# Corrected durations in the planner that orders the instruction streams of a hybrid decoder step

## The chip, the cores and the metric

The kernel runs on one core of one Trainium2 chip. The metric is the device time of one execution in microseconds (us). A core has five engines with a queue each: TensorE (PE) multiplies matrices, VectorE (DVE) and ScalarE (ACT) work element by element, GpSimd (POOL) does the same more slowly and issues the gathers, SyncE (SP) issues most DMAs. Each engine takes its instructions strictly in the order in which the program was written, and waits on semaphores where an operand isn't ready. Matmuls read SBUF and write PSUM, which this kernel uses as eight banks of 128x512 float32.

## The reference

One step of a decoder layer, for a prompt of 1024 tokens and for 8 decode samples of one token with 1024 cached positions:

```python
h = rms_norm(x, norm_g) * (1.0 + scale) + shift          # adaLN of c
proj = h @ w_in                                          # q, 6 k/v, gates, z_a, u, v, z_b, g_a, g_b
o_c, o_s, o_w = nsa_core(...)    # compressed, top-8 selected blocks of 64, window of 512; per-head gates
s_b = spatial_mix(vn, w_s, b_s)  # causal mix in chunks of 128
a = (o_a * silu(z_a)) @ w_br_a
b = (u * s_b * silu(z_b)) @ w_br_b
m = sigmoid(g_a) * a + sigmoid(g_b) * b
y = x + gate * (m @ w_out)
```

Beside y it returns the new K/V rows, the window buffers and the normalised v rows. The samples gather their cached K/V pages by a page table. All is float32.

## The kernel before, in words

Float32 accuracy comes from splitting an operand into a rounded high part and a low remainder (names ending in h and l), and multiplying three times (high by high, high by low, low by high) in the form `float32r`. These are the "split" matmuls of the change. Transposes and a few small products run in plain float32 ("full"), and 16 products of a raw 512-column weight slice with the 9 columns of c ("part" in the change) open the program (`mm<-graw,cT`, `mm<-araw,cT`).

The work has these stages, in the order of the profile:

- Start: the weights of the adaLN are streamed in, x is normalised, transposed and modulated into hh and hl.
- Projections: vg, k, q and v of the prompt (`bh`, `bl`, `gh`, `gl` are their split weights).
- Decode (names gk, gw, kh, kl, psT): for 8 samples, key and value pages of 512 KB are gathered by POOL into four buffers `gk`. For each sample PE transposes the eight 128x128 blocks of a gathered key page in two groups of four (`mx<-main,gk`), ACT rounds each group (`kh<-mx`), DVE takes the remainder (`kl`), and two 512-column matmuls (`st<-kh,qpad`, `st<-kl,qpad`) give the scores. DVE also sums the compressed pages (`red<-gk`). Then come the window pages (`gw`), a softmax, and the products with the values.
- Attention of the prompt: 16 tiles of 128 queries (two groups of heads, eight blocks). Per tile a front part (maxima of the scores by `mx<-L,R` matmuls that DVE reduces into `bm` and `wm`, then the selection), and per span of 128 keys a score pair (`st<-R,L`), an exponential on ACT (`pt<-st`), a mask on POOL, the split into p, and three matmuls on V (`pv<-p,vv`). A tile is closed by sums that go out through DRAM and come back (`sr`, `s`, `w_d`, `f`), a product `mx<-pgT,vc`, and a store to `o_d`.
- Merge: `xh`, `xl` are the split products of z and o (`zt<-z_db`, `zx<-o_d`), multiplied with w_br_b and w_br_a (matmuls `xh,c0h` and so on), gated, summed, split again; then the output projection (`oh`, `ol`).

Beside decode and attention runs a stream of independent jobs, the filler: the projections u, z_a, z_b and the 16 gates, 28 jobs of three pieces. A piece is 24 split matmuls of 344 columns on hh and hl with a chunk of weights (`mm<-hh,c0h`, `mm<-hl,c0h`, `mm<-hh,c0l`; c1 for every other chunk), offered six matmuls at a time, with a tanh on ACT at its end (`th<-mm`) and a store (`t_da<-th` for the last gates). There are 84 pieces, and the merge can't start before all of them are issued, since it is the next job of the same stream.

What decides the order of all this is the class `Plan`. The source is a set of Python generators, one for each stream. As each instruction is written out, `Plan.op` books it on a model of its engine with a duration from `Plan.cost`, and so keeps for each engine the time at which it is free and for each tile the time at which it is ready. `Plan.go` picks, at each step, the generator to continue: first those whose next operand the model calls ready by the time the model's PE is free, among these the one of lowest rank. The filler has rank 9, so it is taken when nothing else is ready in the model. The function `paced` limits the filler during attention by the share of spans done. Nothing of this runs on the chip: the model only fixes in which order the instructions stand in the queues. Every instruction is written out through one line of `Plan.engine`, line 217, so all rows of the profile carry L217.

Of the kernel before, what the change touches and what calls it, by code (L numbers as in the profile page):

```python
# [9 lines left out]
F32 = mybir.dt.float32  # L10
FR = mybir.dt.float32r
BF = mybir.dt.bfloat16
# [16 lines left out]
class Pack:  # L29


    def __init__(self):
        self.cols, self.parts, self.n = {}, [], 0
# [59 lines left out]
class Plan:  # L93
# [6 lines left out]
    def __init__(self):  # L100
        self.free, self.bus, self.slots, self.rings, self.seen = {}, 0.0, {}, {}, {}
        self.columns, self.streams, self.last = {}, [], 0.0
        self.gone, self.since, self.spilled = 0.0, {}, {}

    def tile(self, pool, uid, shape, dtype, name, bufs=1):
        t = pool.tile(shape, dtype, name=name, tag=name, bufs=bufs)
        n = self.rings.get((uid, name), 0)
        self.rings[uid, name] = n + 1
        self.slots[t.tensor.name] = (uid, name, n % bufs)
        return t  # L110
# [54 lines left out]
    def cost(self, engine, name, outs, ins, size, start):  # L165
        if engine == "pe":
            n, m, dt = ins[1].free_size(), ins[0].free_size(), ins[0].dtype
            cost, passes = max(n / 2.4 + 2.5, (26 if dt == BF else 104) * m / 128), 1
            if name == "transpose":
                passes = 2  # L170
            elif dt == F32:
                cost, passes = max(4 * n / 2.4, 208 * m / 128), 4
            tick = int(start // self.TICK)
            self.columns[tick] = self.columns.get(tick, 0.0) + passes * n * ins[0].partition_size() / 128
            return cost * (2 if self.cold(start) else 1)
        if engine == "dve":
            plain = name == "tensor_copy" and outs[0].space == ins[0].space
            return 67 + (0.52 if plain else 1.042) * size
        if engine == "act":
            return (280 if len(ins) > 1 else 70) + 0.834 * size  # L180
        if name == "affine_select":
            return 65 + 1.4 * size
        if name == "tensor_scalar":
            return max(330 + 0.83 * size, 3.61 * size - 28)
        return (300 + 165 * size if size < 16 else 70 + 2.27 * size)
# [1836 lines left out]
```

## Time and profile before

| | |
|---|---|
| median of 3 runs | 1063.16 us (1062.73 to 1066.06) |
| profiled execution | 1060.27 us, its span 1058.5 us |
| PE busy | 1010.8 us (95%) |
| DVE, ACT, POOL busy | 693.9 us (66%), 469.2 us (44%), 307.6 us (29%) |
| granted TensorE clock, mean | 0.991 |

Time idle on PE is what to look for: where PE is busy at full clock, only its own work counts. A row of a timeline gives the start and the length of an instruction; matmuls overlap, so their pitch is the difference of two starts. A table of windows gives the busy time of each engine in a stretch, and the granted clock as a share of 2.4 GHz.

### The profile page before, as it was taken

What the parts mean: (1) busy time and instruction counts of PE and PEld (TensorE: products, weight loads), DVE (VectorE), ACT (ScalarE), POOL (GpSimd) and SP (SyncE); (2) the same over time, 40 slices, a digit from 0 to 9 for tenths busy, and PEclk for the clock granted to TensorE, in tenths of its full rate; (3) what the DMA queues carried; (4) which work ended last, traced back from release to release, by engine and by line L of the source; (5) the groups of instructions that cost most, each with busy time, mean ns of one, the idle gap of its engine ahead of it and who ended that gap; (6) DMA issues with size and microseconds to landing.
All of it is one profiled execution on the core that took longest, in us unless ns stands there. A gap on an engine that the chain in (4) does not pass through costs nothing. (4 is left out here: it accounts for less than half of the span.)

```text
span 1058.5 us, 16280 instructions
## 1 busy us (share of the span) xinstructions
PE 1010.8 (95%) x5587; PEld 875.9 (83%) x5587; DVE 693.9 (66%) x1507; ACT 469.2 (44%) x984; POOL 307.6 (29%) x332
## 2 busy tenths in 40 slices
PE   7999999999999999999999999998999859999998
PEld 2589977879999999988886788877878849998776
DVE  5677786344668665679789867989774146674322
ACT  5763332002222255667765666765776232232000
POOL 0453565463321110013433222342434200252000
PEclk9999999999999999999999999999999979999999
DMA  9726360115766654421322121111112278553421
GB/s 329 260 85 193 115 198 31 60 36 162 261 193 194 223 174 157 129 63 60 86 61 60 61 61 46 55 61 43 36 49 61 81 230 251 169 178 123 139 89 62
DMA packets 106312, 130.33 MB, mean 123 GB/s; under 512 B 27299, under 2 KB 71525, under 8 KB 106230
## 3 DMA queue, kind: packets, MB, share of 16 engines
q1 hardware_dynamic: 101622, 112.52, 33.5%
q0 software_dynamic: 4608, 16.78, 5.2%
q8 instruction: 44, 0.72, 0.3%
q14 instruction: 38, 0.31, 0.1%
HBM read 98.95 MB, written 30.23 MB: 122 GB/s over the span
## 5 line engine op out<-in xcount | busy, mean ns | idle before, releaser
L217 PE MATMUL pv<-p,vv 128*128 128x512 f32 (+1 forms) x396 | 112.7, 400 | 3.5 <-ACT p L217 2.1
L217 PE MATMUL mm<-hh,c0h 128*128 128x344 f32 x328 | 107.7, 328 | 0.0
L217 PE MATMUL mm<-hl,c0h 128*128 128x344 f32 x328 | 105.2, 321 | 0.0
L217 PE MATMUL mm<-hh,c0l 128*128 128x344 f32 x328 | 105.2, 321 | 0.0
L217 PE MATMUL mm<-hh,c1h 128*128 128x344 f32 x320 | 104.3, 326 | 0.0
L217 PE MATMUL mm<-hl,c1h 128*128 128x344 f32 x320 | 102.1, 319 | 0.0
L217 PE MATMUL mm<-hh,c1l 128*128 128x344 f32 x320 | 102.1, 319 | 0.0
L217 ACT ACTIVATE pt<-st 128x512 f32<-128x512 f32 x132 | 78.6, 595 | 50.2 <-PE st L217 45.2
L217 PEld LDWEIGHTS pv<-p,vv 128*128 128x128 f32 (+1 forms) x396 | 65.9, 172 | 27.2 <-DVE p L217 2.6
L217 PE MATMUL st<-R,L 128*128 128x512 f32 (+1 forms) x264 | 85.5, 405 | 0.0
L217 DVE TENSOR_TENSOR p<-pt,p 128x512 fp32r<-128x512 f32 x88 | 67.1, 770 | 12.6 <-ACT p L217 12.1
L217 POOL TENSOR_TENSOR p<-pt,p 128x512 fp32r<-128x512 f32 x44 | 58.9, 1340 | 56.2 <-ACT p L217 49.7
L217 ACT ACTIVATE p<-pt 128x512 fp32r<-128x512 f32 x94 | 59.1, 629 | 14.0 <-POOL pt L217 11.6
L217 PEld LDWEIGHTS mm<-hh,c0h 128*128 128x128 f32 x328 | 62.3, 190 | 2.9 <-issue 0.2
L217 PEld LDWEIGHTS mm<-hh,c0l 128*128 128x128 f32 x328 | 62.2, 190 | 2.6
L217 PEld LDWEIGHTS mm<-hh,c1h 128*128 128x128 f32 x320 | 60.2, 188 | 2.7 <-issue 0.2
L217 PEld LDWEIGHTS mm<-hh,c1l 128*128 128x128 f32 x320 | 60.2, 188 | 2.5
L217 PEld LDWEIGHTS mm<-hl,c0h 128*128 128x128 f32 x328 | 62.1, 189 | 0.0
L217 POOL TENSOR_SCALAR_AFFINE_SELECT pt<-pt 128x512 f32<-128x512 f32 x40 | 27.1, 678 | 116.0 <-ACT pt L217 99.0
L217 PE MATMUL mx<-L,R 128*128 128x512 f32 (+3 forms) x204 | 54.2, 336 | 6.7 <-DVE wm L217 3.0
L217 PEld LDWEIGHTS mm<-hl,c1h 128*128 128x128 f32 x320 | 60.1, 188 | 0.0
L217 ACT ACTIVATE th<-mm 128x344 f32<-128x344 f32 x69 | 31.3, 454 | 52.0 <-PE mm L217 51.7
(489 smaller groups left out, 2657.5 us busy)
## 6 DMA issues: line engine op xcount, KB each, us to landing
t_db<-th SPq DMA_DIRECT2D x24, 172.0 KB
t_da<-th SPq DMA_DIRECT2D x24, 172.0 KB
th<-t_db SPq DMA_DIRECT2D x24, 172.0 KB
th<-t_da SPq DMA_DIRECT2D x24, 172.0 KB
graw<-in_w_ada_dram SPq DMA_DIRECT2D x16, 256.0 KB
araw<-in_w_ada_dram SPq DMA_DIRECT2D x16, 256.0 KB
xt<-in_x_dram SPq DMA_DIRECT2D x8, 512.0 KB
eraw<-in_w_ada_dram SPq DMA_DIRECT2D x16, 256.0 KB
```

The costliest lines, as they stand in the source:

```text
L217: r = getattr(real, name)(*args, **kw)
```

## The change

The constants of `Plan.cost` are replaced, and the model keeps which form the last matmul had, with a time for each change of form. Nothing else in the source is changed. The diff:

```diff
--- before.py
+++ after.py
@@ -101,6 +101,7 @@
         self.free, self.bus, self.slots, self.rings, self.seen = {}, 0.0, {}, {}, {}
         self.columns, self.streams, self.last = {}, [], 0.0
         self.gone, self.since, self.spilled = 0.0, {}, {}
+        self.form = "split"
 
     def tile(self, pool, uid, shape, dtype, name, bufs=1):
         t = pool.tile(shape, dtype, name=name, tag=name, bufs=bufs)
@@ -165,19 +166,32 @@
     def cost(self, engine, name, outs, ins, size, start):
         if engine == "pe":
             n, m, dt = ins[1].free_size(), ins[0].free_size(), ins[0].dtype
-            cost, passes = max(n / 2.4 + 2.5, (26 if dt == BF else 104) * m / 128), 1
-            if name == "transpose":
-                passes = 2
-            elif dt == F32:
-                cost, passes = max(4 * n / 2.4, 208 * m / 128), 4
+            form, passes, turn = "split", 1, 0.0
+            if dt == FR and name != "transpose":
+                cost = max(0.4375 * n + 7, 104 * m / 128)
+                turn = {"split": 0.0, "full": 85.0, "part": 190.0}[self.form]
+            elif name == "transpose" or dt == BF:
+                form, passes = "full", 2 if name == "transpose" else 1
+                cost = max(0.4375 * n + 7, (26 if dt == BF else 104) * m / 128)
+                turn = 190.0 if self.form == "part" else 0.0
+            elif m <= 64 and n > 128:
+                form, passes, cost = "part", 4, 0.4375 * n * 4 * m / 128 + 3
+                turn = 0.0 if self.form == "part" else 140.0
+            else:
+                form, passes, cost = "full", 4, max(4 * (0.4375 * n + 7), 208 * m / 128)
+                turn = 190.0 if self.form == "part" else 0.0
+            self.form = form
             tick = int(start // self.TICK)
             self.columns[tick] = self.columns.get(tick, 0.0) + passes * n * ins[0].partition_size() / 128
-            return cost * (2 if self.cold(start) else 1)
+            return cost * (2 if self.cold(start) else 1) + turn
         if engine == "dve":
             plain = name == "tensor_copy" and outs[0].space == ins[0].space
+            if name == "reciprocal":
+                return 80 + 18 * size
             return 67 + (0.52 if plain else 1.042) * size
         if engine == "act":
-            return (280 if len(ins) > 1 else 70) + 0.834 * size
+            moved = ins and self.box(ins[0])[1][0] != self.box(outs[0])[1][0]
+            return (280 if len(ins) > 1 else 70) + 0.834 * size + (105 if moved else 0)
         if name == "affine_select":
             return 65 + 1.4 * size
         if name == "tensor_scalar":
```

So in the model a split matmul of 344 columns goes from 145.8 to 157.5 ns and one of 512 columns from 215.8 to 231.0 ns, a split matmul after a plain one gets 85 ns more, one of the 16 raw products goes from 853 to 66 ns (with 140 ns in front of it and 190 ns behind it), a reciprocal is dearer the more columns it has, and an ACT instruction that writes other partitions than it reads gets 105 ns more.

The programs have the same instructions, 5462 matmuls and transposes among them, and the changes of form on PE are nearly the same in number: 58 from plain to split in attention in both, 31 in decode in both. What differs is where the filler stands. Counted in pieces of 24 matmuls in PE's order:

| filler pieces issued by | before | changed |
|---|---|---|
| first PE instruction of decode | 3.00 | 2.50 |
| first transpose of a gathered page | 4.75 | 4.00 |
| end of decode | 34.25 | 28.00 |
| first score matmul of attention | 42.50 | 37.00 |
| last matmul on V | 78.00 | 67.50 |
| first matmul of the merge | 84.00 | 84.00 |

The first place is ACT at the end of decode's loop over the key pages; `kh` is one group of four transposed blocks, `th` the end of a filler piece, `c0h` or `c1h` the rounding of half a weight chunk for filler, `kch` the first instruction behind the loop. Before:

```order
L217 ACTIVATE th_3062<-mm_3008 128x344
L217 ACTIVATE c0h_3080<-cr_3004 128x512
L217 ACTIVATE c0h_3080<-cr_3006 128x512
L217 ACTIVATE kh_3091<-mx_3086 128x512
L217 ACTIVATE kh_3121<-mx_3116 128x512
L217 ACTIVATE th_3127<-mm_3067 128x344
L217 ACTIVATE kh_3150<-mx_3145 128x512
L217 ACTIVATE kh_3180<-mx_3175 128x512
L217 ACTIVATE th_3186<-mm_3132 128x344
L217 ACTIVATE kh_3213<-mx_3208 128x512
L217 ACTIVATE kch_3248<-mx_3246 128x256
```

And in the changed kernel:

```order
L231 ACTIVATE c1h_2951<-cr_2866 128x512
L231 ACTIVATE c1h_2951<-cr_2868 128x512
L231 ACTIVATE kh_2968<-mx_2963 128x512
L231 ACTIVATE kh_2992<-mx_2987 128x512
L231 ACTIVATE kh_3018<-mx_3013 128x512
L231 ACTIVATE kh_3042<-mx_3037 128x512
L231 ACTIVATE kh_3065<-mx_3060 128x512
L231 ACTIVATE kh_3096<-mx_3091 128x512
L231 ACTIVATE kh_3119<-mx_3114 128x512
L231 ACTIVATE th_3137<-mm_3080 128x344
L231 ACTIVATE kch_3151<-mx_3149 128x256
```

Three filler pieces end among the last five groups before, and one among the last seven in the changed kernel. On PE 12 and 12 filler matmuls stand around the two groups of a page before, and 12 and 6 in the changed kernel.

The second place is SP behind the last tile of attention; `o_d` is that tile's store, `zt<-z_db` the first loads of the merge, `t_da_140` and `t_da_141` the stores of the last two of 16 gates, `cr` a weight chunk. Before:

```order
L217 DMA o_d_93<-u 128x128
L217 DMA o_d_94<-u 128x128
L217 DMA zt<-z_db_130 128x344 x3
L217 DMA t_da_140<-th 128x344 x2
L217 DMA cr<-in_w_br_b_dram 128x512 x2
L217 DMA t_da_141<-th 128x344 x2
L217 DMA zt<-z_db_131 128x344 x3
L217 DMA t_da_141<-th 128x344
```

And in the changed kernel:

```order
L231 DMA o_d_93<-u 128x128
L231 DMA o_d_94<-u 128x128
L231 DMA zt<-z_db_130 128x344 x3
L231 DMA t_da_137<-th 128x344
L231 DMA cr<-in_w_ga_dram 128x512 x2
L231 DMA zt<-z_db_131 128x344
L231 DMA t_da_138<-th 128x344
L231 DMA zt<-z_db_131 128x344 x2
```

Behind the last store of a tile, two pieces of the seventh and three of the last gate job of branch a are still to be stored before, and the next chunk is one of w_br_b. In the changed kernel one piece of the fourth (t_da_137) and all three of each later gate job follow, and the next chunks are of w_ga.

## Rows read from the trace of the kernel before

**Rows 1.** The page: span, and busy time of each engine with its share.

```profile
span 1058.5 us, 16280 instructions
...
PE 1010.8 (95%) x5587; PEld 875.9 (83%) x5587; DVE 693.9 (66%) x1507; ACT 469.2 (44%) x984; POOL 307.6 (29%) x332
```

**Rows 2.** Windows: key pages of decode, window pages of decode, attention.

```profile
core 0: us, PE busy (x) PEld busy (x) DVE busy (x) ACT busy (x) POOL busy (x), PEclk, DMA share, GB/s
...
258.80:314.80 56.00, 55.42 (x364) 53.54 (x365) 36.68 (x47) 16.48 (x31) 15.23 (x16) 1.00 0.74 243
314.80:365.50 50.70, 50.64 (x329) 49.06 (x327) 39.65 (x68) 14.80 (x29) 9.14 (x8) 1.00 0.65 206
...
454.00:825.00 371.00, 352.19 (x1911) 299.36 (x1911) 293.64 (x700) 250.11 (x529) 126.58 (x140) 1.00 0.19 58
```

**Rows 3.** Windows around the end of attention and the start of the merge.

```profile
823.00:828.00 5.00, 4.20 (x15) 3.62 (x16) 0.00 (x0) 1.46 (x4) 1.28 (x1) 0.66 0.36 113
...
847.00:865.00 18.00, 6.40 (x29) 4.53 (x27) 5.63 (x11) 5.59 (x13) 0.00 (x0) 0.72 0.80 250
865.00:870.00 5.00, 4.71 (x20) 4.66 (x21) 2.56 (x6) 2.26 (x5) 0.00 (x0) 0.64 0.65 179
```

**Rows 4.** Waits of PE from 820 to 873 us: total, times, longest.

```profile
PE st L217 <- ACT xh L217: 9.2, 3, 6.4
...
PE pv L217 <- ACT p L217: 2.1, 1, 2.1
```

**Rows 5.** Timeline of PE, last matmuls on V to the merge: start, length, what.

```profile
820.19 0.86 PE L217 MATMUL pv<-p,vv 128*128 128x512 f32 x3
823.17 0.73 PE L217 MATMUL pv<-p,vv 128*128 128x512 f32 x2 [2.12 <-ACT p L217]
...
825.12 0.49 PE L217 MATMUL mm<-hh,c0h 128*128 128x344 f32 x1
...
827.66 0.32 PE L217 MATMUL mm<-hh,c0h 128*128 128x344 f32 x1
...
849.67 0.32 PE L217 MATMUL mm<-hl,c1h 128*128 128x344 f32 x1
...
869.22 0.32 PE L217 MATMUL mx<-xh,c0h 128*128 128x344 f32 x1
```

**Rows 6.** Chain that ended last: start, length, what.

```profile
873.15 1.89 PE st L217 x12
...
973.77 5.57 PE mm L217 x24
```

**Rows 7.** Timeline of PE in decode's loop over the key pages.

```profile
267.97 0.60 PE L217 MATMUL mx<-main,gk 128*128 128x128 f32 x4
...
270.98 0.60 PE L217 MATMUL mx<-main,gk 128*128 128x128 f32 x4
...
273.77 0.60 PE L217 MATMUL mx<-main,gk 128*128 128x128 f32 x4
...
277.44 0.63 PE L217 MATMUL mx<-main,gk 128*128 128x128 f32 x4 [0.50 <-DMA gk<-in_cache_k_slc_dram,idx]
```

**Rows 8.** Timeline of POOL there: a gather of a page.

```profile
268.84 0.94 POOL L217 DMA_INDIRECT gk<-in_cache_k_slc_dram,idx  x1 [1.33 <-PE mx L217]
```

**Rows 9.** Instructions on gk: gathers from issue to landing.

```profile
DMA to landing us min/median/max: 4.1/5.1/8.5
```

**Rows 10.** Waits of PE in attention, 454 to 820 us.

```profile
PE mx L217 <- DVE bm L217: 6.5, 8, 1.8
PE mx L217 <- DVE wm L217: 4.3, 6, 1.7
```

**Rows 11.** Costliest group of DVE in attention: count, busy, mean ns; idle before.

```profile
L217 DVE TENSOR_TENSOR p<-pt,p 128x512 fp32r<-128x512 f32 x88 | 67.1, 770 | 12.6 <-ACT p L217 12.1
```

**Rows 12.** Instructions on p, DVE: ns min, median, max.

```profile
L217 DVE TENSOR_TENSOR p<-pt,p x88: 674/684/1793, 456.7 to 818.4; 128x512 fp32r<-128x512 f32 x88
```

**Rows 13.** Timeline of PE at the start: a raw product, two records of one instruction.

```profile
26.98 1.02 PE L217 MATMUL mm<-graw,cT 128*9 128x512 f32 x2
```

## The prediction

> **What bounds the kernel now.** I read the page's head first: PE is busy for 1010.8 of 1058.5 us, no other engine for more than 694 [rows 1]. So the kernel is bound by PE's own work, and the place to look at is the 47.7 us in which PE is not busy, with the stretches in which it is busy at a low clock. A table of windows then says where these lie. Decode has almost none (55.42 of 56.00 us and 50.64 of 50.70 us), attention has 371.00 - 352.19 = 18.8 us at a granted clock of 1.00 [rows 2]. The largest hole is behind attention: from 847 to 865 us PE is busy for 6.40 of 18.00 us, and the granted clock falls to 0.72 and then 0.64; a smaller one lies at 823 us, with 0.66 [rows 3]. The waits name the cause: PE waits for ACT's `xh`, the first operand of the merge, 9.2 us in three waits, and before that 2.1 us for the last p of attention [rows 4].
>
> The timeline sizes both holes. At full pitch a split matmul of 344 columns takes 1.89 / 12 = 0.1575 us and one of 512 columns 5.57 / 24 = 0.232 us [rows 6], read in the merge and in the output projection. First hole: from 820.19 to 827.66 us stand six matmuls on V and nine of filler, 6 x 0.232 + 9 x 0.1575 = 2.8 us of work in 7.5 us, 4.7 us lost. Second hole: the last filler matmul begins at 849.67 us and is paced out at 849.83, the merge runs at full pitch from 869.22, and between them stand 24 matmuls of 344 columns, 3.8 us of work in 19.4, 15.6 us lost [rows 5]. Together 20.3 us.
>
> **The change part by part.** It alters no instruction, only the order, and the changes of matmul form stay 58 in attention and 31 in decode. PE's work is therefore the same, and the time moves only by what PE waits and by its clock. I go through the stages by where the filler went; a piece is 24 x 0.1575 = 3.78 us.
>
> *Behind attention.* The merge's first loads can't be ready sooner than about 865.4 us (869.22 - 3.8), 40 us after the last matmul on V (about 825.1 us), since the closing of the last tile and the reloads lie between. Before, 84 - 78 = 6 pieces, 22.7 us, stand there. Changed, 84 - 67.5 = 16.5 pieces, 62.4 us, do. The second hole is covered with 22 us to spare, and on SP the loads `zt<-z_db` still go out right behind the last store of attention, interleaved with filler stores whose tanh is done long before the merge. The first hole is thinned out as well, since filler now stands between the last spans; I leave 1.3 us of it. Gain 19.0 us; bounds 15.6 (the first hole stays whole) and 20.3.
>
> *Decode.* From the first page to the end 34.25 - 4.75 = 29.5 pieces stood before, 24.0 stand now: 20.8 us less to cover the same chain. In the loop over the key pages one sample takes 273.77 - 267.97 = 5.80 us, with 24 filler matmuls in it; with 18 it takes 4.86 us [rows 7]. A page's buffer is free with the transposes at 267.97, the gather goes out at 268.84 [rows 8], and the page is wanted two periods later less the 2.79 us between the two groups of a page (270.98 to 273.77): 7.9 us after the issue before, 6.1 us with the shorter period. The median landing is 5.1 us, the longest 8.5 [rows 9], and the page issued at 268.84 let PE wait until 277.44, 8.6 us later [rows 7]. So the cost is nothing if pages land at the median, and up to 7 x (8.6 - 6.1) = 17.5 us if seven later pages all come like this one. The median is the nearer row, but the DMA engines are 0.74 busy here [rows 2] and the same bytes come in a shorter time, so I take 4. In the window pages 258 filler matmuls become 198, 9.4 us less: PE's 50.6 us become 41.2 against DVE's 39.65 [rows 2], so DVE is nearly the bound; 0 to 4 us, I take 2. Decode loses 6 us; bounds 0 and 21.5.
>
> *Attention.* 78.0 - 42.5 = 35.5 pieces become 67.5 - 37.0 = 30.5, 18.9 us less cover. DVE's 293.64 us [rows 2] are then 83% of 352 us instead of 79% of 371. Its queue is what PE waits for: `bm` and `wm`, the maxima in PSUM banks that PE needs back, 6.5 + 4.3 = 10.8 us [rows 10]. If these waits grow as DVE's free share falls (0.21 to 0.17), they become 13.3 us; with some more for p, whose distance from its scores also shrinks, I take 4 us lost. Bounds: a gain of 5 (a truer order halves the 10.8 us) and a loss of 18.9 (the stage doesn't get shorter at all).
>
> *Start and projections.* One number of the diff is not what the trace shows: a raw product of 9 columns lasts 1.02 us [rows 13], and the model now books 66 ns, at most 140 + 190 ns more for the turns. With 16 of these the model's PE runs up to 16 x 0.62 = 10 us early in the opening stage. There the queues change by one group of transposes here and there; I take 0, between -2 and +5.
>
> The sum: -19.0 + 6 + 4 + 0 = -9.0 us. Against the profiled execution of 1060.27 us that is 1051.3. The median of the runs lies 2.9 us above that execution, so on the median of 1063.16 it is 1054.2 us.
>
> One rule is to be weighed against this. The granted clock fell to a mean of 0.66 after the waits at 820 to 825 us, and nine filler matmuls took 2.54 us instead of 1.42, 1.1 us lost [rows 3, 5]; in attention, with waits up to 1.8 us, it stayed at 1.00 [rows 2, 10]. The Trainium skill, "TensorE: Matmul & The Clock Gate", section "HAM oscillation — how this bites in real kernels", says that a kernel whose PE keeps idling between groups of matmuls has its clock throttled again at each of them. By that rule thinner filler brings more such spells in decode and attention, and five of them at 1.1 us would leave -3.5 us of the -9; by the rows of attention there are none, and I count none.
>
> **The rivals.** *VectorE sets attention* (the slower side). If DVE's queue, not PE's, is the chain there, the stage keeps its 371 us and the filler taken out turns into waits of PE: 18.9 instead of 4. Sum -19.0 + 6 + 18.9 = +5.9, 1069 us. It outweighs the gain from 13 us of new waits in attention on. For it: the waits on `bm` and `wm`, and that the model still books 67 + 1.042 x 512 = 600 ns for the remainder of p, where DVE took 770 ns in the mean [rows 11]. Against it: DVE is not busy for 21% of the stage [rows 2]. Its long cases show in the same operation, 684 ns in the median and 1793 at the longest [rows 12]. The Trainium skill, "SBUF — State Buffer", section "SBUF: two separate sides", says that DVE and GpSimd share a port pair which one holds for a whole instruction while the other blocks. The trace agrees in that this operation has such long cases; by the rule the 88 x 86 ns = 7.6 us between mean and median remain in the changed order, and the model doesn't book them.
>
> *The gathers take back the gain.* If five of seven pages come as late as the one shown, decode loses 12.5 + 2 and attention 4: -0.5, 1062.7 us. For it: that wait, in a loop that had more cover. Against: the median landing.
>
> *The truer order also waits less.* Nothing lost in decode, 5 us won in attention: -24, 1039 us. For it: 18.8 us of waits in attention are there to be won; against it: cover is taken out, not added.
>
> *The corrections miss the trace.* The raw products above put the opening out of order and cost 5 us: -4, 1059 us. For it: the 1.02 us against 66 ns; against it: a model that is early there delays nothing that isn't ready.
>
> **How the numbers follow.** About 0.3%, 3.2 us, is what can be told from no change here. The forecast has 0.58, with a range of its own from 1046 to 1061 us (decode and attention together 2 to 16 us worse); VectorE 0.13, the gathers 0.13, less waiting 0.11, the corrections 0.05. The 80% range from 1043 to 1068 us leaves out the far part of the third rival and about half of the first. Faster: 0.55 of the forecast's 0.58, 0.11 of the third rival and 0.03 of the fourth, 0.69. The same: 0.03, 0.10 of the gathers and 0.02, 0.15. Slower: 0.13 and 0.03 of the gathers, 0.16.
>
> **What would show it.** Right: in the changed profile no wait of PE for `xh` ahead of the merge and a clock of 1.00 through it; about 62 us between the last matmul on V and the merge; the last matmul on V about 33 us earlier than 825 us; new waits of PE of some 4 us on gathered pages and some 14 us on `bm` and `wm`. Wrong: a last matmul on V that is less than 20 us earlier, with waits on `bm`, `wm` and p above 24 us (VectorE), or over 12 us of waits on `gk` (gathers); a wait of PE at the merge in spite of the filler; waits in the first 80 us that the trace of before does not have.

## The result, and the profile after

The changed kernel takes 1069.74 us (median of 8 runs, 1067.30 to 1074.66) against 1062.95 us for the kernel before (8 runs, 1060.60 to 1066.06): ratio 1.0065, 95% interval 1.0043 to 1.0086. It is slower by 0.4 to 0.9%, where 1054 us was forecast. The page's head of the changed kernel's profiled execution, against [rows 1]:

```profile
span 1066.8 us, 16303 instructions
...
PE 1017.3 (95%) x5587; PEld 873.6 (82%) x5587; DVE 697.2 (65%) x1507; ACT 469.3 (44%) x984; POOL 308.8 (29%) x332
```

PE executes the same 5587 instructions and is busy 6.5 us longer, and idle for 49.5 us instead of 47.7. (A matmul counts as busy for its whole length, 0.32 us for one of filler at a pitch of 0.1575 [rows 5, 6], so a short halt and a low clock lie in part in the busy time.) So the hole behind attention was not simply won: something was lost elsewhere. To see where, I cut both traces at the same six instructions: the first projection matmul, decode's first transpose of `qs`, its last (of `tm`), the first score matmul, the last product on V, the first matmul of the output projection. The output projection is counted to PE's last matmul. First the windows of the kernel before (columns as in [rows 2]):

```profile
0.00:39.60 39.60, 32.46 (x113) 10.05 (x113) 22.27 (x46) 23.19 (x41) 5.41 (x12) 1.00 0.90 318
39.60:249.70 210.10, 208.32 (x1091) 178.71 (x1088) 135.95 (x314) 68.03 (x148) 111.07 (x112) 1.00 0.34 107
249.70:414.40 164.70, 162.55 (x1077) 157.22 (x1076) 113.97 (x201) 57.34 (x128) 32.33 (x32) 1.00 0.65 209
414.40:454.20 39.80, 39.29 (x260) 38.10 (x260) 23.30 (x64) 25.20 (x63) 1.97 (x7) 1.00 0.45 129
454.20:824.50 370.30, 351.51 (x1909) 298.69 (x1907) 293.47 (x699) 249.94 (x528) 126.58 (x140) 1.00 0.19 58
824.50:956.90 132.40, 120.12 (x730) 117.55 (x730) 69.65 (x130) 37.19 (x65) 28.04 (x28) 0.94 0.58 176
```

The same six stages of the changed kernel:

```profile
0.00:44.10 44.10, 34.11 (x117) 10.34 (x117) 22.82 (x47) 22.77 (x42) 8.50 (x15) 0.96 0.84 285
44.10:255.40 211.30, 208.48 (x1074) 177.67 (x1072) 133.74 (x313) 67.40 (x147) 110.82 (x109) 0.99 0.35 107
255.40:404.10 148.70, 143.42 (x939) 137.02 (x938) 107.93 (x191) 53.13 (x120) 31.04 (x32) 0.99 0.67 218
404.10:449.80 45.70, 42.09 (x272) 40.30 (x273) 25.42 (x66) 25.77 (x63) 1.87 (x7) 1.00 0.44 122
449.80:809.40 359.60, 337.65 (x1792) 278.52 (x1791) 296.88 (x699) 246.01 (x520) 127.46 (x140) 1.00 0.18 52
809.40:965.40 156.00, 154.97 (x985) 154.22 (x984) 74.65 (x137) 45.74 (x85) 26.41 (x27) 1.00 0.58 177
```

A stage that got shorter has not gained if filler left it. So each difference is read beside the filler: its length, less 3.78 us for each piece (24 filler matmuls of 0.1575 us) that moved. "Loss" below is that number; the pieces are counted in the timelines of PE.

| stage | before: us, pieces | after: us, pieces | loss, us | predicted |
|---|---|---|---|---|
| opening | 39.6, 0 | 44.1, 0 | +4.5 | 0 for these two |
| projections | 210.1, 3.0 | 211.3, 2.5 | +3.1 | |
| decode | 164.7, 31.25 | 148.7, 25.5 | +5.7 | +6 |
| tm to first score | 39.8, 8.25 | 45.7, 9.0 | +3.1 | not counted |
| attention | 370.3, 35.5 | 359.6, 30.5 | +8.2 | +4, less what of the first hole lies here |
| behind attention | 132.4, 6.0 | 156.0, 16.5 | -16.1 | -19.0 with all of the first hole |
| output projection | 96.6, 0 | 96.6, 0 | 0 | 0 |

The sum is +8.5 us against a difference of the spans of 8.3. The boundary behind attention lies where the timeline's row of the last products on V starts. That row holds one product in the kernel before and three in the changed one, so by the last product itself attention loses 0.5 us more, and the stage behind it gains as much more.

A ledger compares one profiled execution with one. That of before took 1060.27 us, while the kernel's medians beside the experiments below are 1064.42 to 1065.84: only one of the 91 executions there took less. So the losses sum to more than the medians differ (8.5 us here against 6.8). What this does to attention's row is told with e2 below. (The first decode row of [rows 2] began at the first page and that of attention ended at 825 us; the cuts here are finer.)

The hole is gone, as forecast. Behind attention no wait for `xh` is left, and this window, which covers the place of [rows 3], is full at a clock of 1.00:

```profile
820.00:880.00 60.00, 60.00 (x385) 60.00 (x384) 25.09 (x48) 23.01 (x49) 2.16 (x3) 1.00 0.65 200
```

Attention's waits of PE, against [rows 10], rose from 10.8 to 15.8 us, close to the "some 14" of the prediction:

```profile
PE mx L231 <- DVE bm L231: 8.5, 11, 2.3
PE mx L231 <- DVE wm L231: 7.3, 15, 0.8
```

VectorE's costliest group there, against [rows 11] (mean 770 ns), and the same operation's spread, against [rows 12]:

```profile
L231 DVE TENSOR_TENSOR p<-pt,p 128x512 fp32r<-128x512 f32 x88 | 73.4, 844 | 11.2 <-ACT p L231 10.9
```
```profile
L231 DVE TENSOR_TENSOR p<-pt,p x88: 674/684/1781, 454.0 to 804.1; 128x512 fp32r<-128x512 f32 x88
```

The median stays 684 ns and the mean rises by 74 ns, 6.3 us over the 88: more long cases, on the engine that PE waits for. The windows of decode's key pages and window pages, against the first two of [rows 2], are 7.5 and 8.1 us shorter for 9.4 us less filler each, the first at a granted clock of 0.96 instead of 1.00:

```profile
265.10:313.60 48.50, 47.57 (x306) 45.56 (x305) 32.22 (x38) 15.36 (x29) 15.24 (x16) 0.96 0.76 254
313.60:356.20 42.60, 41.84 (x270) 39.59 (x269) 36.98 (x64) 12.75 (x25) 7.92 (x8) 1.00 0.81 255
```

The gathers land much as before ([rows 9]):

```profile
DMA to landing us min/median/max: 4.1/5.5/7.7
```

PE waits for a page only once, and 2.5 us for a reduction of VectorE:

```profile
PE mx L231 <- DVE red L231: 2.5, 1, 2.5
PE mx L231 <- DMA gk<-in_cache_k_slc_dram,idx: 0.9, 1, 0.9
```

What the prediction put at zero is the opening. Its first 53 us before (two windows), then the same of the changed kernel:

```profile
0.00:26.00 26.00, 19.41 (x66) 6.15 (x66) 13.84 (x29) 13.52 (x23) 1.33 (x6) 1.00 0.94 328
26.00:53.00 27.00, 26.36 (x124) 15.90 (x124) 18.62 (x42) 20.87 (x43) 12.15 (x18) 1.00 0.76 262
```
```profile
0.00:26.00 26.00, 17.97 (x57) 5.54 (x58) 11.84 (x25) 12.03 (x21) 1.71 (x6) 0.93 0.88 305
26.00:53.00 27.00, 23.81 (x93) 10.93 (x92) 17.46 (x38) 17.80 (x37) 11.28 (x15) 0.94 0.73 235
```

PE gets through 31 matmul records fewer in the second window, at a granted clock of 0.94. The changed kernel's timeline of PE shows how:

```profile
14.71 0.41 PE L231 MATMUL mx<-main,mrow 9*128 9x9 f32 x4 [0.93 <-DVE mrow L231]
...
16.80 0.65 PE L231 MATMUL mm<-gl,cs 128*42 128x512 f32 x1 [0.30 <-DVE gl L231]
...
29.27 1.02 PE L231 MATMUL mm<-graw,cT 128*9 128x512 f32 x2
...
35.45 0.42 PE L231 MATMUL mm<-gh,cs 128*42 128x512 f32 x1 [0.87 <-ACT gh L231]
...
43.76 0.41 PE L231 MATMUL mx<-main,mrow 9*128 9x9 f32 x4 [0.71 <-ACT hx L231]
44.10 0.45 PE L231 MATMUL st<-bh,hh 128*128 128x408 f32 x1
```

The planner books a raw product at 66 ns (it lasts 1.02 us here as in [rows 13]), and small transposes and products now stand where their operands aren't there yet. PE waits, and behind these waits, at 16.80 us, a product of 512 columns takes 0.65 us instead of 0.42. Before, the raw product of [rows 13] starts at 26.98 us and the next one 0.86 us later, so the old booking of 853 ns was nearly right:

```profile
27.84 1.02 PE L217 MATMUL mm<-araw,cT 128*9 128x512 f32 x2
```

### The profile page after: what moved, and what is told of

Its sections match the earlier page's. It is cut to its first block, busy times and chain, and to the rows that moved or that the text cites. A ratio compares the mean times of both kernels' runs of the same rounds, so it can differ in the third digit from the quotient of the medians.

```text
span 1066.8 us, 16303 instructions
## 1 busy us (share of the span) xinstructions
PE 1017.3 (95%) x5587; PEld 873.6 (82%) x5587; DVE 697.2 (65%) x1507; ACT 469.3 (44%) x984; POOL 308.8 (29%) x332
## 5 line engine op out<-in xcount | busy, mean ns | idle before, releaser
L231 PE MATMUL mm<-hh,c1h 128*128 128x344 f32 x304 | 99.5, 327 | 0.0
L231 PE MATMUL mm<-hh,c1l 128*128 128x344 f32 x304 | 97.7, 321 | 0.0
L231 PE MATMUL mm<-hh,c0h 128*128 128x344 f32 x296 | 96.4, 326 | 0.0
L231 PE MATMUL mm<-hh,c0l 128*128 128x344 f32 x296 | 94.6, 319 | 0.6 <-DVE c0l L231 0.6
L231 PE MATMUL mm<-hl,c0h 128*128 128x344 f32 x296 | 94.5, 319 | 0.0
L231 DVE TENSOR_TENSOR p<-pt,p 128x512 fp32r<-128x512 f32 x88 | 73.4, 844 | 11.2 <-ACT p L231 10.9
L231 PE MATMUL mx<-L,R 128*128 128x512 f32 (+3 forms) x204 | 56.6, 344 | 10.4 <-DVE wm L231 4.1
L231 ACT ACTIVATE p<-pt 128x512 fp32r<-128x512 f32 x94 | 59.1, 629 | 15.9 <-POOL pt L231 12.5
L231 POOL TENSOR_TENSOR m<-m,th 128x344 f32<-128x344 f32 x24 | 24.8, 1053 | 119.9 <-DMA th<-t_da 96.3
L231 PEld LDWEIGHTS mm<-hh,c0l 128*128 128x128 f32 x296 | 55.7, 188 | 3.3 <-DVE c0l L231 0.9
L231 PEld LDWEIGHTS mm<-hh,c0h 128*128 128x128 f32 x296 | 55.7, 188 | 2.8 <-issue 0.4
L231 PEld LDWEIGHTS mx<-L,R 128*128 128x128 f32 x204 | 34.4, 188 | 26.7 <-PE mx L231 5.1
```

The source lines that it names most:

```text
L231: r = getattr(real, name)(*args, **kw)
```

## The experiments

All kernels ran in five rounds beside the kernel before, whose median was 1064.42, 1064.97, 1064.80 and 1065.84 us in the four groups (e1 to e4, e5 to e8, e9 to e12, e13 to e15). The table has each median and ratio, attention's length and pieces, and the losses by stage as above (the profiled execution's, against that of before). Times of different groups are compared by their ratios. By the last product on V itself, and not its row, attention loses 0.5 us more in all of them but e2, and 1.4 in e3, e4 and e6.

| run | median us | ratio, 95% | attention us, pieces | opening and projections | decode | to first score | attention | behind |
|---|---|---|---|---|---|---|---|---|
| changed kernel | 1069.74 | 1.0065 [1.0043, 1.0086] | 359.6, 30.5 | 7.6 | 5.7 | 3.1 | 8.2 | -16.1 |
| e1 | 1065.94 | 1.0019 [1.0000, 1.0038] | 360.6, 30.5 | 4.6 | 5.9 | 2.8 | 9.2 | -17.2 |
| e2 | 1071.98 | 1.0073 [1.0047, 1.0099] | 375.2, 35.5 | 10.4 | -0.3 | 0.0 | 4.8 | 2.0 |
| e3 | 1060.70 | 0.9973 [0.9957, 0.9989] | 371.0, 31.5 | 1.2 | -0.5 | 0.0 | 15.8 | -14.2 |
| e4 | 1080.42 | 1.0148 [1.0123, 1.0173] | 371.5, 27.5 | 1.1 | 0.2 | 0.0 | 31.4 | -8.0 |
| e5 | 1053.50 | 0.9898 [0.9876, 0.9919] | 341.2, 30.5 | 9.5 | 6.3 | 3.4 | -10.3 | -16.3 |
| e6 | 1064.95 | 1.0003 [0.9983, 1.0024] | 353.5, 27.5 | 1.4 | 1.0 | -0.3 | 13.4 | -9.5 |
| e7 | 1060.66 | 0.9963 [0.9948, 0.9979] | 372.1, 32.0 | 0.0 | -0.1 | 2.2 | 15.0 | -15.9 |
| e8 | 1059.58 | 0.9948 [0.9932, 0.9965] | 356.4, 31.0 | 8.0 | 4.9 | 1.9 | 3.0 | -15.8 |
| e9 | 1067.46 | 1.0026 [1.0009, 1.0043] | 368.3, 31.0 | 0.2 | 5.1 | 3.5 | 15.0 | -16.0 |
| e10 | 1063.05 | 0.9980 [0.9964, 0.9997] | 365.6, 31.5 | 1.1 | 4.9 | 3.8 | 10.3 | -15.6 |
| e11 | 1055.98 | 0.9922 [0.9902, 0.9943] | 355.2, 29.75 | 0.4 | -0.7 | 1.3 | 6.6 | -17.3 |
| e12 | 1066.35 | 1.0010 [0.9995, 1.0025] | 373.6, 35.75 | 9.4 | 6.6 | 2.1 | 2.3 | -12.3 |
| e13 | 1054.53 | 0.9900 [0.9874, 0.9926] | 370.0, 34.0 | 0.7 | 0.1 | 1.0 | 5.3 | -14.9 |
| e14 | 1057.62 | 0.9926 [0.9904, 0.9947] | 360.3, 30.0 | 1.0 | -0.3 | 1.8 | 10.8 | -15.0 |
| e15 | 1058.42 | 0.9931 [0.9911, 0.9952] | 362.7, 30.75 | 1.6 | 0.6 | 1.8 | 10.3 | -15.9 |

**e1 and e2: the raw products.** e1 is the changed kernel with the raw product booked near what it takes; e2 is the kernel before with only this booking spoilt.

```diff
 e1
 ...
-                form, passes, cost = "part", 4, 0.4375 * n * 4 * m / 128 + 3
-                turn = 0.0 if self.form == "part" else 140.0
+                form, passes, cost = "split", 4, 4 * n / 2.4
 ...
 e2
 ...
+            elif dt == F32 and m <= 64 and n > 128:
+                cost, passes = 0.4375 * n * 4 * m / 128 + 3, 4
             elif dt == F32:
                 cost, passes = max(4 * n / 2.4, 208 * m / 128), 4
 ...
```

> The changed kernel with one number put back: a raw product of 9 columns is booked with 853 ns as before, and without a turn. Filler counts stay those of the changed kernel (28.0 pieces by the end of decode, 67.5 by the last matmul on V); only the opening and a few places behind it move. Theory A, the mis-booked raw products cost the 4.5 us that the opening lost (first projection matmul at 44.1 us instead of 39.6): that matmul comes back to 39.6 to 40.5 us, and the whole is 4 to 5 us below the changed kernel, about 1065 us. Rival B, any shift of the model disorders the opening: it stays at 43 to 45 us, and the whole at 1068 to 1071 us.

> The kernel before with only the raw products mis-booked, 66 ns instead of 853 and no turns. Filler counts as before (34.25 and 78.0). Theory A: the first projection matmul comes at 43 to 45 us and the whole is 4 to 5 us above the kernel before, about 1067 us. Rival B: 39 to 41 us, and 1062 to 1064 us.

Theory A is right on the opening: 39.2 us in e1, 44.2 in e2. The one booking makes the kernel before 7.6 us slower in the median, as much as opening and projections lose in the changed kernel. But in e1 part of it is lost again in the projections (213.3 us with 2.5 pieces, a loss of 5.0): the other corrections spoil the projections too. e1's median lies 3.8 us below the changed kernel's, and 5.3 us when each is taken against the kernel before beside it. The openings of e1, with its clock back, and of e2:

```profile
0.00:39.20 39.20, 31.71 (x105) 9.30 (x105) 20.71 (x43) 21.63 (x39) 3.90 (x11) 1.00 0.90 316
```
```profile
0.00:44.20 44.20, 34.17 (x108) 10.29 (x108) 22.04 (x45) 22.29 (x41) 7.46 (x14) 0.96 0.83 284
```

e2 also shows how far two executions of one order differ. From 180 us on the instructions of PE, VectorE and ScalarE stand in the order of the kernel before, and yet attention and the stage behind it take 4.9 and 2.0 us longer:

```profile
464.20:839.40 375.20, 354.52 (x1909) 299.49 (x1908) 297.62 (x699) 250.16 (x529) 127.62 (x140) 0.99 0.19 57
839.40:973.80 134.40, 120.82 (x729) 118.42 (x730) 69.72 (x130) 36.63 (x65) 27.58 (x28) 0.93 0.57 174
```

This execution took 4.9 us more than e2's median, that of before some 4 us less than its own. So up to 5 us of a loss in attention's column can be the choice of the execution; the column is better read from run to run than against zero. The stages ahead of decode agree far better: in the eleven profiles that share the order of before there, the opening lies within 39.1 and 40.9 us and the projections within 209.9 and 211.0.

**e3 and e4: filler taken out, old durations.** The kernel before, with 4 or 8 pieces held back for the time behind attention:

```diff
-    SPANS, PACE_LEAD, PACE_FRONT, PACE_REST = 132, 12, 14, 6
+    SPANS, PACE_LEAD, PACE_FRONT, PACE_REST = 132, 12, 14, 10     (e4: 14)
```

> The kernel before with one constant changed, PACE_REST from 6 to 10: old durations, opening and decode word for word as before, but 10 instead of 6 pieces are left behind the last matmul on V (4 x 3.78 = 15.1 us, against 15.6 us lost in the hole there). Theory C, cover: a piece taken out of attention gives back only a part, since VectorE's queue is behind; the changed kernel lost about 11 us there for 5 pieces, 2.2 each, so 8.8 are lost here and 14 to 15 won behind it: 1056 to 1058 us. Rival D, margin: the loss came from the new durations, which place each operation with less to spare; with the old ones attention loses under 3 us: 1050 to 1052 us. Rival E, VectorE sets attention wholly: it keeps its length, and nothing is won, 1063 us.

> As the run before, with PACE_REST at 14: 8 pieces (30.2 us) are taken out of attention, only about 4 of them are needed behind it. Theory C: the hole is closed (15 to 16 us won), attention loses 8 x 2.2 = 17.6: about 1064 us. Rival D: attention loses 6 at most: 1053 us. Rival E: attention keeps its 370 us and the surplus filler adds 30.2 - 15.6 = 14.6 us: 1077 us.

Attention takes 371.0 and 371.5 us, as with all its filler: 15.1 and 30.2 us of work are taken out, and in these executions nothing is gained. The medians are a little kinder: with the hole's 14.2 and 8.0 us they leave some 11 of the 15.1 us lost and some 24 of the 30.2 (an estimate from these numbers). So e3's time lies between theories C and E, and e4's 3 us above E's. In e3 the hole pays for it, in e4 no longer. Windows of e4, two of 20 us and attention as a whole, against the last row of [rows 2]:

```profile
620.00:640.00 20.00, 16.38 (x79) 12.30 (x80) 14.19 (x27) 16.38 (x34) 8.32 (x8) 1.00 0.14 36
640.00:660.00 20.00, 16.04 (x62) 12.08 (x60) 14.69 (x34) 10.75 (x24) 3.23 (x4) 0.74 0.08 23
455.40:827.00 371.60, 337.16 (x1716) 273.93 (x1715) 293.25 (x693) 243.76 (x516) 125.30 (x140) 0.96 0.17 50
```

PE's busy time falls by 14.3 us only (351.5 to 337.2), not by 30.2: the granted clock is 0.96 in the mean, where it was 1.00, and 0.74 in the stretch behind a stretch with PE idle for 3.6 us. 4% of 371.6 us are 14.9, nearly the 15.9 that are missing. The filler had covered waits and, in this stage, kept the clock at its upper level.

**e5 and e6: less work for VectorE.** The changed kernel and e4's, each in its own order, but the maxima over score blocks read half of each block's columns (this leaves half of the scores out of the maxima). The planner still books them whole, by lines that the diff here leaves out.

```diff
 ...
             dve.tensor_reduce(dst[:, c * 128 // width:(c * 128 + n) // width],
-                              b[:, :n].rearrange("p (a x) -> p a x", x=width), op=OP.max, axis=AX.X)
+                              b[:, :n].rearrange("p (a x) -> p a x", x=width)[:, :, 0:width // 2], op=OP.max, axis=AX.X)
 ...
```

> The changed kernel, in the same order on every engine, but the maxima over the score blocks (bm and wm) read only the first half of the columns of each block: VectorE has some 132 reductions of about 0.27 us less, about 35 us in attention, and the output is no longer the reference's. Theory E (VectorE and what waits for it sets the length of attention): the waits for bm and wm, 16.0 us in the changed kernel, fall under 5 us, and attention goes from 359.6 to 343-350 us; the time to about 1055 us (1050-1060). Rival T (attention lasts as long as TensorE's own work and filler, and its waits only change their name): attention 357-361 us and 1067-1071 us.

> The kernel before with eight pieces of filler moved behind attention (the kernel of e4_rest14, whose attention stayed at 371.6 us), with the same halved maxima and the order otherwise untouched; again the output is not the reference's. Theory E: attention falls from 371.6 by 15-30 us, to 342-356, since it has 30.2 us less filler and now 35 us less for VectorE; the time from 1080.4 to 1050-1065 us. Rival T': something else than VectorE (ScalarE, GpSimd or the gathers of rows) kept attention at 371 us when filler was taken out: attention stays 368-372 us and the time 1077-1083 us.

Theory E is right in both, 341.2 and 353.5 us, 18 us less each (341.2 is even below its range), and by the ratios the times are 18 and 15 us lower. The work of PE and the order on every engine are unchanged, so this shows that VectorE's queue holds attention up. Its waits, and attention's window, in e5:

```profile
PE mx L232 <- DVE bm L232: 2.7, 4, 1.0
PE mx L232 <- DVE wm L232: 1.5, 4, 0.6
```
```profile
452.60:793.80 341.20, 332.50 (x1793) 279.79 (x1792) 262.99 (x698) 245.13 (x520) 128.96 (x140) 1.00 0.19 55
```

VectorE does 34 us less there (296.9 to 263.0) and half of that comes back as time: its queue holds PE up at some places and not throughout.

**e7 and e12: where the corrected durations pay.** The old cost function stays as `old_cost`, and a flag chooses. e7 takes the old one up to decode's end and the corrected one behind it; e12 the other way round.

```diff
 ...
+    def cost(self, *args):
+        return (self.old_cost if self.old else self.new_cost)(*args)
 ...
     plan.go(until=lambda: "decode" in over and jobs_done[0] >= b_jobs)
+    plan.old = False          (e12: False from the start, True here)
 ...
```

> The old durations through opening, projections and decode, the corrected ones from the end of decode on: up to the end of decode the order is the one of the kernel before, with 34.25 pieces by then; 73.25 pieces by the last V product instead of 78 (67.5 in the changed kernel). Theory S (the loss is made ahead of attention, the corrected durations pay in attention): first projection matmul at 39-41 us, decode 164-166 us, attention 360-364 us, 10.75 pieces behind it that fill the hole of 16 us, 133-136 us from the last V product to the first output matmul; the time 1055 us (1051-1059), faster than the kernel before by 4-12 us. Rival L (attention was shorter in the changed kernel only because it came with fewer pieces done, and keeps 368-372 us here): 1060-1066 us.

> The complement of e7_attention_only: corrected durations to the end of decode (28 pieces there, as in the changed kernel), the old ones behind it: 38.5 pieces at the first score matmul, 74.25 by the last V product, so 35.75 in attention (before 35.5, changed kernel 30.5), and 9.75 behind it for the hole. Theory V: opening, projections and decode lose their 13 us as in the changed kernel, attention takes 368-373 us as in the kernel before, with its filler under cover (the changed kernel lost 8 us there), and the hole gives 14-16 us back: 1058-1064 us, below the changed kernel. Rival D (the corrected durations are what holds attention at 360 us): the same 13 us lost and attention longer by its 5 pieces without a gain: 1068-1074 us.

Rival L's numbers came, 1060.66 us and an attention of 372.1 us: 3.5 pieces were taken out of it and it got no shorter. The first of these windows shows that the clock falls as in e4. But over the whole of attention, the second, it is 0.99, and 1% of 372.1 us is 3.7, so this is a part of the 15.0 us and not all:

```profile
480.00:500.00 20.00, 17.35 (x86) 14.27 (x86) 16.55 (x34) 11.55 (x26) 5.77 (x6) 0.91 0.08 23
451.50:823.60 372.10, 348.73 (x1826) 287.40 (x1825) 299.46 (x696) 244.68 (x521) 126.69 (x140) 0.99 0.18 53
```

In e12 attention loses only 2.3 us with its filler back, as theory V has it, but the opening and projections lost 9.4 (7.6 in the changed kernel, with the same order), and 1066.35 us lies between the two ranges. So theory S, that the corrected durations pay in attention, falls; what gains in both is the hole behind it.

**e8 to e11: the pitch alone, and the place where the new numbers begin.** e8 is the kernel before with one line changed. e9 has all corrections, and e10 the pitch alone, from the hand-over behind the projections on; e11 the pitch alone from the end of decode on.

```diff
 ...
-            cost, passes = max(n / 2.4 + 2.5, (26 if dt == BF else 104) * m / 128), 1
+            cost, passes = max(0.4375 * n + 7, (26 if dt == BF else 104) * m / 128), 1
 ...
```

> The kernel before with the pitch of TensorE's matmuls corrected (0.4375 n + 7 ns in place of n/2.4 + 2.5) and nothing else: 31.25 pieces by the end of decode (34.25 before, 28 in the changed kernel), 68.75 by the last V product (78 and 67.5). Theory P (the pitch moves the filler, and the raw products cost the opening): first projection matmul at 39-41 us, decode loses 2-4 us against its filler, attention 358-363 us, the time 1055-1061 us. Rival N (the terms for a change of form and for ScalarE are what makes attention shorter): attention 368-372 us with the filler gone, the time 1064-1075 us.

> The old durations through opening and projections, all corrected ones from the hand-over to decode on: 3.0 pieces of filler at decode's start as in the kernel before, 32.25 at its end, 39.5 at the first score matmul, 70.5 by the last V product (before 78, changed kernel 67.5). Theory O (the term of the prediction that failed first is the zero for opening and projections, +7.6 us in the changed kernel, and the stages behind it keep their own sums): first projection matmul 39-41 us, projections 209-212, decode 2-5 us longer than its filler accounts for, attention 31 pieces in 358-364 us, 133-136 us behind it beside the filler that fills the hole; the time 1055-1062 us, 8-14 us below the changed kernel. Rival R (what the opening loses in the changed kernel is only work put off, so that it comes back later): 1065-1071 us.

> Old durations through opening and projections, then only the pitch of matmuls corrected: 32.25 pieces at decode's end, 70.5 by the last V product, as in e9. Theory O: the loss of 7.5 us that e8_pitch_only had in its projections is gone and its attention (31 pieces in 356 us) stays: 1052-1057 us. Rival C (an attention of 356 us was one lucky order, and another order with as much filler takes 360-372 us): 1057-1066 us. Against e9 it also tells whether the terms for a change of form and for ScalarE add anything from decode on: within 2 us of e9 if not.

> Old durations up to the end of decode, then only the pitch: 34.25 pieces there (no loss in decode), 40.75 at the first score matmul, 70.5 by the last V product: 29.75 pieces in attention, 5.75 fewer than before. Theory V (VectorE and the clock hold attention near 360-372 us, whatever filler is taken out): attention 360-370 us, the time 1056-1063 us, no better than e10 although decode loses nothing. Rival F (attention shortens with its filler, since in e8 it did): 350-356 us and 1046-1053 us.

Theory P holds for e8's time, its attention is shorter still, and the pitch alone moves the filler. It did not foresee that projections lose 7.5 us there. e9 has the opening and projections of before, 7.4 us less loss than the changed kernel, and its time is only 2.3 us lower (4.1 us, each taken against the kernel before beside it), in rival R's range: 6.8 us came back as loss in attention (15.0 for 8.2). Whether the lost time is put off, as R says, or another order draws other waits, these two kernels don't tell. e10 mends e8's projections, and again attention is worse (365.6 us, 10.3 us lost for 3.0): 1063.05 us, rival C. It is 4.4 us below e9, so here the other terms cost that much from decode on. e11 loses 1.0 us ahead of attention and fills the hole, and is faster than before by 0.6 to 1.0%. Its attention of 355.2 us is in rival F's range, its time between the two, so it decides for neither; its profiled execution lies 5.7 us below its median, so the stage lengths flatter it. Its windows for attention and behind it:

```profile
448.60:803.80 355.20, 334.97 (x1775) 275.90 (x1774) 289.66 (x698) 243.63 (x518) 128.57 (x140) 1.00 0.18 53
803.80:947.20 143.40, 143.35 (x912) 142.89 (x912) 72.53 (x135) 43.56 (x78) 26.32 (x27) 1.00 0.61 185
```

**e13 to e15: which term spoils attention's order.** e7's kernel without the term for a change of form (e13), without those for ScalarE and the reciprocal (e14), without either (e15).

```diff
 e13, e15
 ...
-            return cost * (2 if self.cold(start) else 1) + turn
+            return cost * (2 if self.cold(start) else 1)
 ...
 e14, e15
 ...
-            if name == "reciprocal":
-                return 80 + 18 * size
 ...
-            return (280 if len(ins) > 1 else 70) + 0.834 * size + (105 if moved else 0)
+            return (280 if len(ins) > 1 else 70) + 0.834 * size + 0
 ...
```

> The kernel of e7_attention_only (old durations to the end of decode, corrected ones behind it; attention 372 us, 1060.7 us) without the term for a change of matmul form: 75.25 pieces by the last V product, 34 in attention. Theory U (the term for a change of form is what spoils attention's order): what attention loses beyond its filler falls from 15.0 us to 5-8, so attention takes 369-373 us with 34 pieces, and the time is 1053-1058 us (with 8.75 pieces behind it some 3 us of the hole stay open). Rival W (the ScalarE and reciprocal terms spoil it): the loss stays 13-17 us, attention 377-381 us, 1061-1066 us. Rival Q (each order draws its own waits, whatever term made it): anything in between.

> The kernel of e7_attention_only without the terms for ScalarE's partition-moving copies and for the reciprocal: 71.0 pieces by the last V product, 30.0 in attention. Theory U: the loss beyond filler stays 13-17 us, attention 363-367 us, the time 1060-1065 us. Rival W: the loss falls to 5-8 us, attention 355-358 us, the time 1053-1057 us.

> The kernel of e7_attention_only without either: the pitch and the durations of whole and part-width float32 products alone, 71.5 pieces by the last V product, 30.75 in attention. Theories U and W both: the loss beyond filler is e11's, 5-8 us, attention 357-360 us, 1054-1058 us. Rival Q: it differs from e11 by over 3 us although the numbers behind the order are nearly the same.

Attention's loss falls from 15.0 us to 5.3, 10.8 and 10.3. e13 is as theory U has it, e14 and e15 are as neither has it. The term for a change of form costs 9.7 us where ScalarE's stand (e7 to e13) and 0.5 where they don't (e15 to e14). The times agree: without this term 6.7 us are won by the ratios of e7 and e13, and e15 is 0.8 us slower than e14. So no term has a price of its own. That each order draws its own waits, rival Q, fits this, but isn't shown by its own test: e15's attention loses 3.7 us more than e11's, within what executions differ, and by the ratios the times are 1 us apart. e13 is the fastest with all of the work in it, by 0.7 to 1.3% against before; the intervals of e11, e14 and e15 overlap with its own. Its windows for attention and behind it:

```profile
451.20:821.20 370.00, 349.58 (x1875) 291.10 (x1874) 293.88 (x698) 247.09 (x524) 128.74 (x140) 1.00 0.19 54
821.20:949.00 127.80, 126.16 (x798) 124.94 (x798) 67.61 (x131) 38.88 (x69) 25.99 (x27) 1.00 0.64 196
```

## Why the prediction was wrong

Two terms of the sum failed: opening and projections, put at 0 for a reason that was wrong, and attention, whose 4 us were too few. A stretch of 3.1 us was in no term. Of the signs named for being wrong, waits in the first 80 us that the trace of before does not have came (0.9 us for `mrow`, 0.7 for `hx`), and the last matmul on V comes 15 us earlier, not 33, though with 15.8 us of waits on `bm` and `wm` and not 24.

*Behind attention: right.* Of the first hole's 4.7 us, 3.2 lie ahead of the last product on V, in attention's row of the ledger: from 820.19 to 824.53 us are 4.34, with five products of 0.232 in them. So the two holes gave 16.1 + 3.2 = 19.3 us, where 19.0 was forecast. In the runs that had 10 pieces or more behind attention and kept the clock, this stage gained 14 to 17 us.

*Decode: right in its sum, not in its split.* 5.7 us against 6. But the four us put on gathers were one wait of 0.9 us; the rest is VectorE's (2.5 us for `red`), a clock of 0.96 over the key pages and smaller losses. e7 and e11 keep the 31.25 pieces and lose nothing. That the loss is the price of the cover is argued from this, not shown: in e9 two pieces less cost 5.1 us, as much as 5.75 here.

*Attention: failed, mis-sized.* The mechanism was named, DVE's queue with less cover, and its size taken as 4 us with bounds to 18.9. It measured 8.2 us and the 3.2 of the first hole that it had won, 11.4; against e2's execution of the old order 3.4 + 3.2 = 6.6. The waits on `bm` and `wm` came out close to the forecast, 15.8 us for 10.8 (in e1 and e2, the second executions of the two orders, 16.1 and 11.1). Missing was that PE's busy time fell by 13.9 us only where 18.9 of filler left; the other waits hardly changed. Nor is the opening alone to blame: with the opening and projections of before, the other corrections still end at 1067.46 us (e9), in another order, with 15.0 us lost here. The rival that VectorE sets attention names the same chain with a price of 18.9 us: e3 and e4 show most of it or all where cover is taken out, e5 and e6 its cause. In the changed kernel a third to three fifths of that price was paid.

*Opening and projections: failed, a term put at nothing.* This is the miss that stands clear of the scatter of executions. The prediction read that a raw product takes 1.02 us where the model books 66 ns, and took 0, with -2 to +5 as bounds. Its reason, that a model which runs early delays nothing that isn't ready, was wrong: PE works in the order written, so what is placed early and isn't ready holds up what is. These stages lost 7.6 us; e2 shows that this booking alone can do that, e1 that taking it back gives 4.9 us in the opening and 3.8 to 5.3 in the time. What the projections lose with the other corrections (5.0 in e1, 7.5 in e8) was in no step, nor was the stretch from `tm` to the first scores, 3.1 us, where PE's idle time goes from 0.5 to 3.6 us.

*The rules weighed there.* The prediction counted no spells of a low clock in decode and attention. In attention the changed kernel has none (1.00, with waits up to 2.3 us); over decode's key pages its clock is 0.96, and in its opening 0.93 and 0.94; e4 and e7 have such spells in attention (0.74, 0.91). The Trainium skill, "TensorE: Matmul & The Clock Gate", section "HAM oscillation — how this bites in real kernels", says that a PE which idles between groups of matmuls is throttled again and again. The opening, e4 and e7 agree with it, the changed kernel's attention doesn't show it. The Trainium skill, "SBUF — State Buffer", section "SBUF: two separate sides", says that VectorE and GpSimd share a port pair, which one holds for a whole instruction while the other blocks. The long cases of p's remainder would fit that, and they grew (mean 844 ns against 770, median 684 in both), but no run here separates the port from other causes.

*What stays open.* Why one order with 31 pieces in attention loses 3 us (e8) and another 15 (e9). That is more than executions of one order differ. The waits of PE there tell where most of it lies, on `wm`, first e8, then e9:

```profile
PE mx L217 <- DVE wm L217: 3.5, 8, 1.5
PE mx L254 <- DVE wm L254: 13.1, 16, 3.0
```

What in the order makes these waits is open: both hold the same work, and the terms of the model don't sort them. Open too is how much of the changed kernel's loss in attention is scatter, since of the kernel before a single trace is kept.

## What to carry to other kernels

Work that fills time under another engine's chain isn't worth its own length when it is moved: ask, stage by stage, what the time is without it, and take filler out only where the place that it goes to is a real hole. One number of an order's cost model that is wrong by more than ten times does its harm on the engine that works in written order, even where the model errs on the early side. When a table of costs sets an order, each version draws several us of luck (here 12 us between attentions of equal work, of which up to 5 may be the execution), so a forecast of 1% needs bounds of that size, and truer costs alone promise nothing. And a ledger of two profiles needs a second profile of one order beside it, to tell what two executions differ by.

## What the runs showed that was not expected

Moving 30 us of matmuls from attention to the time behind it (e4) made the kernel 16 us slower, and the granted clock fell to 0.74 in one stretch of 20 us. Halving the columns of the maxima over 512 columns took `bm`'s 70 reductions of that form from 689 to 422 ns each in the mean, so 256 columns cost 267 ns (the changed kernel, then e5):

```profile
L231 DVE TENSOR_REDUCE bm<-mx 128x8 f32<-128x512 f32 x70 | 47.9, 689 | 2.0 <-PE mx L231 0.3
L232 DVE TENSOR_REDUCE bm<-mx 128x8 f32<-128x256 f32 x70 | 29.3, 422 | 2.6 <-PE mx L232 0.9
```

And one wrong booking, of products that lie in the first 45 us, cost 7.6 us at the end (e2).
